# Splitting the second block's input weights early, whole-row convolution taps and shared softmax scalings in a two-block layer on one core

## The chip, the cores and the metric

The kernel runs as one program on one core of a Trainium2 chip. A core has engines that work side by side, each through its own instructions in a fixed order: TensorE (PE: matrix products and transposes), VectorE (DVE), ScalarE (ACT), GpSimd (POOL), and SyncE (SP), which here only issues DMA transfers. The metric is the device time of one execution in microseconds (us). Three runs of the kernel before gave 2321.71, 2323.44 and 2327.45 us, so the median is 2323.44 us.

## The reference

A sequence of 1024 tokens of width 1024 (float32) goes through two blocks. The first normalises the tokens, makes four branches of attention and retention (A to D) from one input product, merges them with gates and adds the result to the input. The second block is the part that the change touches:

```
xn = rms_norm_2(h, g_mix_pre)
z  = xn @ w_in                                   # 1024 x 2308
conf_ab, q, k, v, f_logit, sc_h, sc_b, sc_c, pool_v = split(z)
y_conf = silu(layer_norm(conv31(a * sigmoid(b)))) @ w_conf_pw   # 256 channels, 31 taps, causal
y_att  = forgetting_attention(q, k, v, f_logit + b_forget)      # 4 heads of 64, causal
y_sc   = sc_b * conv3(sc_c * sc_h)                              # 256 channels, 3 taps
y_pool = (windowed mean - v) @ w_pool * scale                   # windows 2, 4, 8, 16
h = h + rms_norm_2(concat(y_conf, y_att, y_sc, y_pool) @ w_out, g_mix_post)
# then a gated MLP and a last gated product
```

## The kernel before

**Products in three parts.** TensorE multiplies float32 values that are split into two parts, hi (the value rounded to the engine's float32r type) and lo (the value minus hi). Each product is hi times hi, hi times lo and lo times hi. The names in the rows are `wr` for a raw weight block from DRAM, `wh` and `wl` for its two parts. One product of 128 output channels by 512 tokens is 24 matmuls of 512 columns into one PSUM bank `mm` (lines 229 to 231).

**Weights.** `load_w` (line 184) loads a weight group block by block through SP's queue into slots of the pool `w` (`NW=9` slots of 128 x 1024 floats), and `split_w` makes hi with ACT or DVE in turn (`WHI='aaav'`, line 147 for ACT's copy, 149 for DVE's cast) and lo with DVE (line 157) or POOL (line 155). A block takes a slot for the raw values and one for each part; in the second block's mixing stage lo is always made by DVE (`WLO2='v'`). For the mixing stage the groups are two for the convolution (conf), two for queries and keys (qk0, qk1), one for values (v, 260 columns, 8 tiles of 128 tokens), two times two for the short convolution (sc, sb) and one for the pooling: 20 raw blocks.

**The stages in time.** Branch D at about 110 to 280 us, branch A at 290 to 660 us, branches C and B to 1000 us, the merges and the first output product to 1178 us, mixing from 1178 to 1512 us, then its output product and the MLP. In the mixing stage the text uses three stretches. Stretch one, 1235 to 1290 us, is the products qk0 and v and the start of the short convolution's product. Stretch two, to 1427 us, is the attention of heads 0 and 1 in eight tiles of 128 queries with other products between them. Stretch three, to 1512 us, is the attention of heads 2 and 3 with the end of the convolution's branch and the first output products.

**The 31 taps.** `tap` (line 1334 in the rows; the first of a channel group at 1331) adds one shifted, weighted copy of `u` to an accumulator on DVE, with both inputs in SBUF. There are two channel groups m and two halves of the tokens, and `conv(m, half)` gives 31 taps each, so 124 instructions of up to 512 columns. `conv_steps` takes from these lists: two taps after each product, four after each attention tile (`CPP=2`, `CS=4`), in turn over the lists of one half; `conv_rest` takes what is left before the convolution's branch is used.

**An attention tile.** `softmax_pair` treats two heads: TensorE makes scores (bank `s`), DVE adds the bias and takes the maximum (line 838, `Pm` and `mx`), combines it (843, 847), ACT makes the exponentials (850), DVE takes the reciprocal of the sum (858) and scales both heads' rows (line 150, `Pm<-Pm,sm`). Then TensorE transposes `Pm` (line 276, bank `t`), ACT and DVE split that into `PT`, TensorE multiplies with the values (816), and DVE and ACT join the result (826, 827).

**Order.** The order on each engine is fixed when the program is built: code is placed in priority order, and a helper `stream` moves a part ahead of or behind the rest. The string `WORK` lists the pieces of the mixing stage one after another. The table `FA` says, for each of branch A's 16 attention tiles, which other pieces follow it.

**The short convolution.** `short_conv` (line 1492) makes sc_h and sc_c, copies sc_h from PSUM with ACT, multiplies with DVE, then makes sc_b, which ACT copies from PSUM, runs three taps of 1024 columns and multiplies by the copy (line 1507).

## Time and profile before

| | |
|---|---|
| runs | 2321.71, 2323.44, 2327.45 us |
| profiled execution, its own time | 2326.04 us |
| its span in the trace | 2324.3 us |
| busy, PE / DVE / ACT / POOL | 2235.5 / 1518.4 / 962.6 / 495.1 us |
| mean granted clock of TensorE | 0.989 of full speed |

TensorE works 96% of the span. In a window from 290 to 660 us it is busy all the time, so other engines' work there is beside it. In the mixing stage it is not: it waits between matmuls, and in windows with such waits the granted clock is below 1.00. A row of a window view has each engine's busy time with its count of instructions, then the clock. A row of a timeline has the start, the duration, the engine, the line, the operation with output and inputs, the count, and in brackets how long the engine had been idle and what released it.

### The profile page before, as it was taken

What the parts mean: (1) busy time and instruction counts of PE and PEld (TensorE: products, weight loads), DVE (VectorE), ACT (ScalarE), POOL (GpSimd) and SP (SyncE); (2) the same over time, 40 slices, a digit from 0 to 9 for tenths busy, and PEclk for the clock granted to TensorE, in tenths of its full rate; (3) what the DMA queues carried; (4) which work ended last, traced back from release to release, by engine and by line L of the source; (5) the groups of instructions that cost most, each with busy time, mean ns of one, the idle gap of its engine ahead of it and who ended that gap; (6) DMA issues with size and microseconds to landing.
All of it is one profiled execution on the core that took longest, in us unless ns stands there. A gap on an engine that the chain in (4) does not pass through costs nothing.

```text
span 2324.3 us, 30295 instructions
## 1 busy us (share of the span) xinstructions
PE 2235.5 (96%) x11004; PEld 1853.1 (80%) x11004; DVE 1518.4 (65%) x2952; ACT 962.6 (41%) x1937; POOL 495.1 (21%) x411
## 2 busy tenths in 40 slices
PE   7999999999989999999998998899999999999998
PEld 6788788888887778877887787677788888888877
DVE  7634466665677965634579876855576778678684
ACT  6211344444455544422322344634445454334452
POOL 4222100010155622224320000012043440000021
PEclk9999999999999999999999999999999999999999
DMA  9432221121132333224320211156555687524313
GB/s 326 154 95 63 60 69 50 49 88 60 33 109 85 115 121 105 73 82 147 107 68 26 82 54 34 37 172 206 161 186 187 197 324 252 181 91 155 117 55 118
DMA packets 202783, 272.72 MB, mean 117 GB/s; under 512 B 17086, under 2 KB 126214, under 8 KB 202634
## 3 DMA queue, kind: packets, MB, share of 16 engines
q1 hardware_dynamic: 194240, 257.95, 34.3%
q10 hardware_dynamic: 8394, 12.84, 1.8%
q8 instruction: 87, 1.43, 0.3%
q14 instruction: 62, 0.51, 0.1%
HBM read 199.43 MB, written 71.32 MB: 116 GB/s over the span
## 4 chain that ended last, share of the span: by engine, by line
PE 46%; DVE 6%; DMA 2%; ACT 1%; issue 1%; POOL 0%; SPq 0%; DVEq 0%; POOLq 0%; ACTq 0%
PE mm L230 6%; PE mm L231 6%; PE mm L229 6%; DVE blk L1334 2%; PE s L1676 2%; PE s L1675 2%; PE s L1674 2%; PE t L2020 1%; PE t L2021 1%; PE t L2019 1%; PE t L276 1%; PE mm L2020 1%; PE t L1676 1%; PE t L1675 1%; PE t L1674 1%; PE mm L2021 1%
## 5 line engine op out<-in xcount | busy, mean ns | idle before, releaser
L229 PE MATMUL mm<-blk,wh 128*128 128x512 f32 x1264 | 506.4, 401 | 12.7 <-DVE tz L1149 5.3
L230 PE MATMUL mm<-blk,wh 128*128 128x512 f32 x1264 | 502.1, 397 | 0.9 <-DVE blk L157 0.9
L231 PE MATMUL mm<-blk,wl 128*128 128x512 f32 x1264 | 501.0, 397 | 2.0 <-POOL wl L155 1.7
L229 PEld LDWEIGHTS mm<-blk,wh 128*128 128x128 f32 x1264 | 239.4, 189 | 65.1 <-DVE tz L1149 7.9
L231 PEld LDWEIGHTS mm<-blk,wl 128*128 128x128 f32 x1264 | 239.4, 189 | 52.4 <-POOL wl L155 2.1
L230 PEld LDWEIGHTS mm<-blk,wh 128*128 128x128 f32 x1264 | 239.5, 189 | 47.8 <-DVE blk L157 1.3
L155 POOL TENSOR_TENSOR wl<-wr,wh 128x1024 fp32r<-128x1024 f32 (+1 forms) x50 | 122.9, 2458 | 480.1 <-ACT wh L147 290.2
L229 PE MATMUL mm<-wh,blk 128*128 128x512 f32 (+3 forms) x544 | 197.0, 364 | 7.1 <-DVE wh L149 1.6
L231 PE MATMUL mm<-wh,blk 128*128 128x512 f32 (+3 forms) x544 | 194.3, 359 | 1.0 <-DVE blk L157 1.0
L157 DVE SCALAR_TENSOR_TENSOR wh<-blk,wh 128x1024 fp32r<-128x1024 f32 x116 | 138.6, 1221 | 66.9 <-issue 59.2
L147 ACT ACTIVATE wh<-blk 128x1024 fp32r<-128x1024 f32 x116 | 117.0, 1053 | 154.4 <-PE s L2020 84.5
L230 PE MATMUL mm<-wl,blk 128*128 128x512 f32 (+3 forms) x480 | 170.2, 355 | 9.5 <-DVE wl L157 9.1
L147 ACT ACTIVATE blk<-mm 64x512 fp32r<-64x512 f32 (+3 forms) x138 | 77.9, 569 | 172.0 <-PE mm L231 113.2
L147 ACT ACTIVATE PT<-t 128x512 fp32r<-128x512 f32 (+3 forms) x224 | 96.0, 460 | 118.2 <-PE o L816 65.9
L147 ACT ACTIVATE wh<-wr 128x1024 fp32r<-128x1024 f32 (+2 forms) x91 | 93.7, 1031 | 102.2 <-DMA wr<-in_w_in_dram 21.9
L157 DVE SCALAR_TENSOR_TENSOR PT<-t,PT 128x512 fp32r<-128x512 f32 (+3 forms) x224 | 111.0, 515 | 37.4 <-ACT PT L147 36.4
L309 POOL TENSOR_TENSOR sm<-sm,mhalf 128x1 f32<-128x1 f32 x64 | 38.8, 610 | 437.3 <-DVE sm L308 422.0
L229 PEld LDWEIGHTS mm<-wh,blk 128*128 128x128 f32 x544 | 103.3, 190 | 25.4 <-DVE wh L149 2.4
L231 PEld LDWEIGHTS mm<-wh,blk 128*128 128x128 f32 x544 | 103.4, 190 | 16.8 <-DVE blk L157 1.9
L230 PEld LDWEIGHTS mm<-wl,blk 128*128 128x128 f32 x480 | 91.7, 191 | 24.3 <-DVE wl L157 11.3
L157 DVE SCALAR_TENSOR_TENSOR wl<-wr,wh 128x1024 fp32r<-128x1024 f32 (+2 forms) x69 | 88.5, 1283 | 31.5 <-PE mm L230 14.0
L1150 POOL TENSOR_TENSOR acc<-tz,acc 128x512 f32<-128x512 f32 x48 | 67.8, 1416 | 132.2 <-DVE tz L1149 86.4
(364 smaller groups left out, 4851.5 us busy)
## 6 DMA issues: line engine op xcount, KB each, us to landing
acc<-acc SPq DMA_DIRECT2D x96, 256.0 KB, 2.6
wr<-in_w_merge_dram SPq DMA_DIRECT2D x32, 512.0 KB, 4.0
wu<-in_w_up_dram SPq DMA_DIRECT2D x32, 512.0 KB, 5.1
blk<-in_w_down_dram SPq DMA_DIRECT2D x32, 512.0 KB, 7.0
blk<-ss SPq DMA_DIRECT2D x32, 512.0 KB, 4.7
wr<-in_w_in_dram SPq DMA_DIRECT2D x27, 512.0 KB, 4.2
ss<-us SPq DMA_DIRECT2D x48, 256.0 KB, 2.3
blk<-sa SPq DMA_DIRECT2D x24, 512.0 KB, 4.3
```

The costliest lines, as they stand in the source:

```text
L147: return ac.activation(dst, src, AF.Copy, scale=1.0 if scale is None else scale)
L155: return po.tensor_tensor(lo, x, hi.bitcast(F32), op=ALU.subtract)
L157: return ve.scalar_tensor_tensor(out=lo, in0=x, scalar=scale, in1=hi.bitcast(F32), op0=ALU.mult, op1=ALU.subtract)
L229: pe.matmul(dst, sh, mh, start=(i == 0), stop=False)
L230: pe.matmul(dst, sh, ml, start=False, stop=False)
L231: last = pe.matmul(dst, sl, mh, start=False, stop=(i == n - 1))
L1150: po.tensor_tensor(acc[:], t[:], acc[:], op=ALU.add)
L1334: ve.scalar_tensor_tensor(out=acc[:, c:c1], in0=u[:, c - l:c1 - l], scalar=w, in1=acc[:, c:c1], op0=ALU.mult, op1=ALU.add)
L1674: pe.matmul(dst, wh, xh, start=first and k == 0, stop=False, skip_group_check=True)
L1675: pe.matmul(dst, wh, xl, start=False, stop=False, skip_group_check=True)
L1676: last = pe.matmul(dst, wl, xh, start=False, stop=k == 3, skip_group_check=True)
L2020: pe.matmul(d, sh[:, c, ts_], tl[:, c, :], start=False, stop=False)
```

## The change

Three edits, and one table that orders them.

First, the 20 raw blocks of `w_in_2` are split during branch A. A generator `w2_split` loads a block by SP's queue, makes hi with ACT and lo with DVE, and stores both parts to DRAM by GpSimd's queue. `FA` gains 20 letters `w`, each one such step, over all 16 tiles (one after most tiles, two after five of them). In the mixing stage `load_w2` loads the parts with GpSimd's queue, 40 loads, in place of 20 raw loads by SP's queue, and nothing is split there.

Second, the taps. Group 0's first 16 taps stay in halves, its other 15 and all 31 of group 1 run over whole rows of 1024 columns: 32 + 15 + 31 = 78 instructions. They stand in a stream of their own, placed 150 priorities later (`TAPL=150`), and the lists are taken one after another.

Third, in the mixing attention the scaling of a tile's first head goes to ACT and that of the second stays with DVE (`NORM2='av'`). With these, `short_conv` makes sc_b after its taps and multiplies straight from PSUM, half by half, so that ACT's copies of sc_b go; and two small casts (`identR`, `causR`) come earlier.

```diff
-FA={(0, 2): 'g', (0, 3): 'mmm', (0, 7): 'qm', (1, 0): 'gg', (1, 6): 'gz'} ... NORM2='v'
+FA={(0, 0): 'w', (0, 1): 'w', (0, 2): 'gw', (0, 3): 'mmmw', ... (1, 0): 'ggww', (1, 1): 'ww', ...} ... NORM2='av', TAPL=150
...
     def conv_steps(n):
-        for _ in range(n):
-            if convs:
-                half, steps_ = convs.pop(0)
-                if next(steps_, "end") != "end":
-                    convs.insert(sum(h == half for h, _ in convs), (half, steps_))
+        with stream("taps", tc.tile_snap_priority() + _T["TAPL"]):
+            for _ in range(n):
+                if convs and next(convs[0], "end") == "end":
+                    convs.pop(0)
...
+    def w2_split():
+        for key, (cs_, n, per) in w2_cols.items():
+            N = n * len(cs_)
+            for b in range(KC // per):
+                raw = main.tile([P, per, N], F32, name=nm("wr"), tag="w", bufs=NW)
+                for i, c0 in enumerate(cs_):
+                    sy.dma_start(raw[:, :, i * n:(i + 1) * n], w_in2[:, b * per:(b + 1) * per, c0:c0 + n])
+                hi, lo = [main.tile([P, per, N], F32R, name=nm("wh"), tag="w", bufs=NW) for _ in range(2)]
+                copy(hi[:], raw[:], "a")
+                sub_lo(lo[:], raw[:], hi[:])
+                for j, t in enumerate((hi, lo)):
+                    d = dram.tile([P, per, N], F32R, name=nm("w2"), tag=nm("w2"), bufs=1)
+                    po.dma_start(d[:], t[:])
+                    w2_d[key, b, j] = d
+                yield
...
+    def load_w2(*key):
...
+        for b in range(KC // per):
+            for j, p_ in enumerate((w.h, w.l)):
+                p_[b] = main.tile([P, per, n * len(cs_)], F32R, name=nm("wh"), tag="w", bufs=NW)
+                po.dma_start(p_[b][:], w2_d[key, b, j][:])
...
-    def conv(m, half):
-
-        for l in range(31):
-            tap(accs[m], us[m], l, dwc[:, m, 30 - l:31 - l], l == 0, half * 512, half * 512 + 512)
+    def conv(m, ls, halves=((0, S),)):
+
+        for l in ls:
+            for c0, c1 in halves:
+                tap(accs[m], us[m], l, dwc[:, m, 30 - l:31 - l], l == 0, c0, c1)
             yield
...
     for m in range(2):
         z_half(hT2, first[m], 1, conf_evac[m])
-        convs.append((1, conv(m, 1)))
+        if m == 0:
+            convs.append(conv(0, range(16), ((512, S),)))
+            convs.append(conv(0, range(16, 31)))
+        else:
+            convs.append(conv(1, range(31)))
...
-            z_group(hT2, load_w([(w_in2[:, :, 1540 + m * P:1540 + (m + 1) * P], 0)], 128),
-                    lambda b, j, half: copy(bb[:, half * 512:(half + 1) * 512], b[:], "a"), ms=(0,))
-            for l in range(3):
-                tap(hh_, u, l, dwc[:, m, 33 - l:34 - l], l == 0)
-            ve.tensor_mul(hh_[:], hh_[:], bb[:])
...
+        for l in range(3):
+            tap(y, u, l, dwc[:, m, 33 - l:34 - l], l == 0)
+
+        def times(b, j, half):
+            cs = slice(half * 512, (half + 1) * 512)
+            ve.tensor_mul(y[:, cs], b[:], y[:, cs])
+        z_group(hT2, load_w2("sb", m), times, ms=(0,))
```

Three places show how the order moves. The first is DVE while TensorE makes the v product, in stretch one; `fl` and the 4x64 rows are that product's results, and line 1334 (before) or 1374 (after) is a tap. Before:

```order
L1334 SCALAR_TENSOR_TENSOR blk_11224<-blk_11312,dwc,blk_11224 128x489
L1334 SCALAR_TENSOR_TENSOR blk_11223<-blk_11225,dwc,blk_11223 128x512
L1334 SCALAR_TENSOR_TENSOR blk_11224<-blk_11312,dwc,blk_11224 128x512
L157 SCALAR_TENSOR_TENSOR blk_11674<-mm_11758,blk_11674 128x4x64
L149 COPY fl<-mm_11758 128x4
L1334 SCALAR_TENSOR_TENSOR blk_11224<-blk_11312,dwc,blk_11224 128x488
```

After:

```order
L1374 SCALAR_TENSOR_TENSOR blk_11435<-blk_11437,dwc,blk_11435 128x994
L157 SCALAR_TENSOR_TENSOR blk_11870<-mm_11919,blk_11870 128x4x64
L149 COPY fl<-mm_11919 128x4
L157 SCALAR_TENSOR_TENSOR blk_11871<-mm_11947,blk_11871 128x4x64
L149 COPY fl<-mm_11947 128x4
L157 SCALAR_TENSOR_TENSOR blk_11871<-mm_11975,blk_11871 128x4x64
L149 COPY fl<-mm_11975 128x4
```

Between two tiles of v stood three to six taps; now the last one stands ahead of the second tile's results, and none comes after them.

The second place is DVE in the attention of heads 0 and 1, around the fifth tile's reciprocal (line 858 before, 903 after; 838 or 883 is a maximum, 826 or 871 and 827 or 872 the joining of an earlier tile's result). Before:

```order
L847 TENSOR_TENSOR sm_12385<-mx_12363,c_63 128x2
L838 ISA Pm_12442,mx_12441<-s_12447,xb_12153 128x256
L838 ISA mx_12441 128x1
L858 RECIPROCAL sm_12390<-sm_12387 128x2
L150 TENSOR_SCALAR Pm_12364<-Pm_12364,sm_12390 128x640
L826 TENSOR_REDUCE blk_12157<-o_12305 64x128
L150 TENSOR_SCALAR Pm_12374<-Pm_12374,sm_12390 128x640
L157 SCALAR_TENSOR_TENSOR wl_12984<-wr_12981,wh_12983 128x1024
```

After:

```order
L1374 SCALAR_TENSOR_TENSOR blk_11436<-blk_11518,dwc,blk_11436 128x1010
L1374 SCALAR_TENSOR_TENSOR blk_11436<-blk_11518,dwc,blk_11436 128x1009
L903 RECIPROCAL sm_12566<-sm_12563 128x2
L871 TENSOR_REDUCE blk_12334<-o_12481 64x128
L1374 SCALAR_TENSOR_TENSOR blk_11436<-blk_11518,dwc,blk_11436 128x1008
L150 TENSOR_SCALAR Pm_12550<-Pm_12550,sm_12566 128x640
L872 TENSOR_TENSOR blk_12334<-blk_12334,ju_12528 128x128
L1374 SCALAR_TENSOR_TENSOR blk_11436<-blk_11518,dwc,blk_11436 128x1007
L883 ISA Pm_12627,mx_12616<-s_12628,xb_12332 128x512
```

One scaling and the weight's subtraction left this row of work, and four taps of whole rows came into it. From the reciprocal of the fourth tile to that of the seventh there are 19 such taps after and none before.

The third place is POOL at the end of the first output product, with the norm's power (`sm`, line 309 before, 308 after), the row sums (`row`, 1267 or 1312) and, after, the loads of weight parts (line 694). Before:

```order
L309 TENSOR_TENSOR sm_11105<-sm_11105,mhalf 128x1
L155 TENSOR_TENSOR wl_11237<-wr_11229,wh_11236 128x1024
L1267 TENSOR_TENSOR row_11144<-xt_11142,row_11144 128x512
L309 TENSOR_TENSOR sm_11113<-sm_11113,mhalf 128x1
L155 TENSOR_TENSOR wl_11324<-wr_11316,wh_11323 128x1024
```

After:

```order
L694 DMA wh_11519<-w_581_2951 128x1024
L308 TENSOR_TENSOR sm_11317<-sm_11317,mhalf 128x1
L694 DMA wh_11521<-w_583_2953 128x1024
L694 DMA wh_11523<-w_691_3574 128x1024
L694 DMA wh_11525<-w_693_3576 128x1024
L694 DMA wh_11735<-w_741_3747 128x1024
L1312 TENSOR_TENSOR row_11356<-xt_11354,row_11356 128x512
L308 TENSOR_TENSOR sm_11325<-sm_11325,mhalf 128x1
```

Two subtractions of weights left POOL, and nine loads came, eight of them together; the last row sums stand behind these.

## Rows read from the trace of the kernel before

**Rows 1.** The page: busy time by engine, then the chain's lines.

```profile
PE 2235.5 (96%) x11004; PEld 1853.1 (80%) x11004; DVE 1518.4 (65%) x2952; ACT 962.6 (41%) x1937; POOL 495.1 (21%) x411
...
PE mm L230 6%; PE mm L231 6%; PE mm L229 6%; DVE blk L1334 2%; PE s L1676 2%; PE s L1675 2%; PE s L1674 2%; PE t L2020 1%; PE t L2021 1%; PE t L2019 1%; PE t L276 1%; PE mm L2020 1%; PE t L1676 1%; PE t L1675 1%; PE t L1674 1%; PE mm L2021 1%
```

**Rows 2.** Windows: length, PE, PEld, DVE, ACT, POOL busy, clock, DMA.

```profile
1235.00:1290.00 55.00, 43.83 (x263) 38.74 (x263) 54.59 (x94) 12.29 (x22) 0.00 (x0) 0.91 0.19 49
1290.00:1427.00 137.00, 134.61 (x678) 112.21 (x677) 99.77 (x218) 51.45 (x108) 2.46 (x3) 1.00 0.17 51
1427.00:1512.00 85.00, 71.94 (x361) 55.22 (x360) 71.47 (x199) 49.47 (x112) 4.36 (x7) 0.94 0.11 38
...
1255.00:1260.00 5.00, 1.97 (x7) 1.67 (x8) 4.94 (x8) 0.98 (x2) 0.00 (x0) 0.55 0.39 101
...
1460.00:1470.00 10.00, 8.79 (x35) 5.23 (x34) 9.99 (x30) 10.00 (x21) 0.93 (x1) 1.00 0.00 1
290.00:660.00 370.00, 370.00 (x2050) 319.86 (x2049) 230.91 (x722) 170.33 (x429) 46.16 (x39) 1.00 0.18 58
```

**Rows 3.** The chain of waits that ended last, 1235 to 1300 us, by line.

```profile
by line: DVE blk L1334 60.5%; DVE blk L157 10.3%; PE mm L231 7.6%; PE mm L229 6.7%; PE mm L230 6.5%; DVE wl L157 3.6%; issue 2.1%; PE t L276 1.3%; DVE fl L149 1.1%; DVE wh L149 0.9%
```

**Rows 4.** Timeline of PE, stretch one: its longest wait.

```profile
1256.94 0.58 PE L230 MATMUL mm<-wl,blk 128*128 128x260 f32 x1 [2.93 <-DVE wl L157]
```

**Rows 5.** Timeline of DVE: taps, a cast and a subtraction, stretch one.

```profile
1261.44 5.94 DVE L1334 SCALAR_TENSOR_TENSOR blk<-blk,dwc,blk 128x512 f32<-128x512 f32 x9
...
1281.45 0.69 DVE L149 CAST wh<-wr 128x1024 fp32r<-128x1024 f32 x1
...
1284.41 1.23 DVE L157 SCALAR_TENSOR_TENSOR wl<-wr,wh 128x1024 fp32r<-128x1024 f32 x1
1285.54 0.73 DVE L1334 SCALAR_TENSOR_TENSOR blk<-blk,dwc,blk 128x482 f32<-128x482 f32 x1
```

**Rows 6.** Line 1334 in stretch one, 1235 to 1290 us: count, durations.

```profile
L1334 DVE SCALAR_TENSOR_TENSOR blk<-blk,dwc,blk x64: 710/740/758, 1234.5 to 1289.9; 128x512 f32<-128x512 f32 x37, 128x491 f32<-128x491 f32 x2, 128x490 f32<-128x490 f32 x2, 128x489 f32<-128x489 f32 x2
```

**Rows 7.** Windows in the attention of heads 0 and 1 (columns as above).

```profile
1338.28:1370.32 32.04, 29.65 (x163) 24.53 (x162) 24.65 (x69) 14.71 (x32) 0.00 (x0) 1.00 0.18 50
1290.00:1338.28 48.28, 48.28 (x232) 39.97 (x231) 37.33 (x78) 16.97 (x38) 0.00 (x0) 1.00 0.21 61
```

**Rows 8.** Timeline of DVE there: the fourth and the seventh tile's reciprocal.

```profile
1338.28 0.17 DVE L858 RECIPROCAL sm<-sm 128x2 f32<-128x2 f32 x1 [1.12 <-ACT Pm L850]
...
1370.32 0.16 DVE L858 RECIPROCAL sm<-sm 128x2 f32<-128x2 f32 x1
```

**Rows 9.** Mixing, by line: DVE's scalings and ACT's copies, durations min/median/max.

```profile
L150 DVE TENSOR_SCALAR Pm<-Pm,sm x32: 279/511/754, 1315.6 to 1499.5; 128x128 f32<-128x128 f32 x4, 128x256 f32<-128x256 f32 x4, 128x384 f32<-128x384 f32 x4, 128x512 f32<-128x512 f32 x4
...
L147 ACT ACTIVATE wh<-wr x17: 623/1057/1065, 1177.1 to 1512.0; 128x1024 fp32r<-128x1024 f32 x14, 128x520 fp32r<-128x520 f32 x3
```

**Rows 10.** DMA issues of 1178 to 1512 us: KB, us to landing.

```profile
wr<-in_w_in_dram SPq DMA_DIRECT2D x4, 512.0 KB, 4.3
...
wr<-in_w_in_dram SPq DMA_DIRECT2D x4, 260.0 KB, 3.0
```

**Rows 11.** Timeline of SP's queue, end of the first output product: one issue.

```profile
1171.92 0.34 SPq L1277 DMA_DIRECT2D x<-row  x1
```

**Rows 12.** Timeline of POOL, same place.

```profile
1172.07 2.41 POOL L155 TENSOR_TENSOR wl<-wr,wh 128x1024 fp32r<-128x1024 f32 x1 [1.50 <-ACT wh L147]
1174.43 1.75 POOL L1267 TENSOR_TENSOR row<-xt,row 128x512 f32<-128x512 f32 x1
```

**Rows 13.** Timeline of DVE and of POOL around 1086 us.

```profile
1085.40 2.74 POOL L155 TENSOR_TENSOR wl<-wr,wh 128x1024 fp32r<-128x1024 f32 x1 [1.21 <-DVE wl L157]
...
1085.80 2.90 DVE L149 CAST wh<-wr 128x1024 fp32r<-128x1024 f32 x1
```

**Rows 14.** Timeline of PE: two matmuls of one product, 512 columns.

```profile
1342.03 0.39 PE L231 MATMUL mm<-blk,wl 128*128 128x512 f32 x1
1342.26 0.39 PE L229 MATMUL mm<-blk,wh 128*128 128x512 f32 x1
```

72 lines of the change are left out of this document (44 added, 28 removed).

## The prediction, made before the changed kernel ran

> **What bounds the kernel now.** I read the page first, then windows, then the waits. TensorE is busy 2235.5 of 2324.3 us and leads the chain; the one DVE line in the chain's list that is worth naming is the taps, 2% [rows 1]. So only places where TensorE waits can give time. The windows show two of them in the mixing stage [rows 2]. In stretch one TensorE works 43.83 of 55.00 us while DVE works 54.59: DVE is the bound, and the chain there is 60.5% taps [rows 3]. TensorE's longest wait, 2.93 us, ends on DVE's weight subtraction [rows 4]. The granted clock is 0.91 over the stretch, and in the 5 us in which TensorE worked only 1.97 it was 0.55 [rows 2], so waits are paid a second time. In stretch three TensorE works 71.94 of 85.00 at clock 0.94, DVE 71.47, and ACT 10.00 of 10 us for a while. In stretch two TensorE works 134.61 of 137.00: nearly nothing to gain, and something to lose.
>
> **Stretch one: gain.** At most the idle 55.00 - 43.83 = 11.2 us and the lost clock, 0.09 x 55 = 5.0, together 16. DVE loses 64 taps of a half row [rows 6]. Nine in a row take 5.94 us, 0.66 each; so 64 x 0.66 = 42.2. Three subtractions of 1.23 and about two half-sized, and a cast of 0.69 [rows 5], go too: 3.7 + 1.4 + 0.7 = 5.8. Fifteen taps of a whole row come; a row of that size is followed by the next start 1.13 us later (1284.41 to 1285.54) [rows 5], so 17 us. DVE then has 54.6 - 42.2 - 5.8 + 17 = 24 us of work beside some 44 of TensorE: it is no longer the bound. What is late next is the weights' slots. Of the nine slots the v group takes eight, and the last of them come free only when qk0 ends; sc0's parts wait for v in the same way. A landing took 3.0 us for a v block and 4.3 for a full one from SP's queue [rows 10], and the last product before it covers part. I leave about 2 us of wait for each and 1 for the clock: 5 of the 16 stay. Gain 11, bounds 3 (each wait a full landing and an issue, and more clock) and 16.
>
> **Stretch two: loss.** The taps of channel group 1 that DVE no longer does in stretch one now stand between the pieces of the softmax. I take the stretch from the fourth to the seventh reciprocal, 1338.28 to 1370.32 us [rows 8], because before and after it the order gives TensorE products to work on, and inside it, after the change, there are none for three tiles. Before, DVE works 24.65 of 32.04 us, TensorE 29.65 [rows 7]. Out of DVE go one subtraction (1.23), one cast (0.70) and one scaling of three tiles (about 0.5 each [rows 9]): 21.2 left. In come 19 whole-row taps at 1.13: 21.5. So DVE has 42.7 us of work. TensorE has less than before, since some 5 us of the filling product moved ahead of the stretch: about 24.6. The difference is 18.1. DVE may enter it ahead; the maxima of a tile can't be taken before its scores, so I allow one tile's spare, 3 us. That gives 15 us of waiting where 2.4 stood: +12.7, and +1.3 for the clock after waits of several us (0.55 in the window named above). Loss 14. Bounds: 4, if DVE arrives some 10 us ahead (in the 48.28 us before the stretch it worked only 37.33 [rows 7], 10.9 spare), and 20, if it has no lead and the clock costs more. Between the ends I go nearer the upper one, because the taps before the stretch stand in the same kind of order and eat that spare time.
>
> **Stretch three: gain.** Eight of the scalings leave DVE, 8 x 0.5 = 4 us [rows 9], with two subtractions and a cast, 3 us more; the waits on the softmax shorten by at most that. ACT takes the eight scalings, and there it is at 10.00 of 10 us [rows 2], so part turns into waiting for ACT. Gain 4, bounds 0 and 12 of the 13.1 idle and 5.1 of clock. The moved scalings of stretch two are counted above; ACT has 51.45 of 137 there, and there they cost nothing.
>
> **The short convolution.** ACT loses four copies per half pair; DVE does two products of half a row from PSUM in place of one whole row, in stretches two and three, where the sum above already lies within the bounds. I cost it at 0; without that cover it is half a microsecond.
>
> **The start of mixing.** Nine loads go to GpSimd's in-order queue; behind eight of them stand the last row sums, the first of which began at 1174.43 [rows 12]. No row shows an issue by GpSimd: the nearest from below is SP's, 0.34 us [rows 11], from above the longest POOL operation there, 2.41 [rows 12]. Eight give 2.7 to 19 us from about 1166, when the first slots come free. Two subtractions of that kind leave POOL in return. I take a value near SP's, as both only start a transfer: the sum is 1 to 2 us later and covered by the convolution's product, which TensorE has ready. With the wait for the first parts I set +1, bounds 0 and 8. A value below nothing is excluded: TensorE did not wait there.
>
> A page speaks against the parts' way through GpSimd. In this trace a cast of 128 x 1024 took 0.69 us alone [rows 5] and 2.90 us while POOL subtracted beside it [rows 13]. The Trainium skill, page "SBUF — State Buffer", section "Who interferes with whom", says that a DVE instruction with two SBUF inputs contends with GpSimd instructions that read SBUF, and that a transfer which DVE seems to stall was one whose descriptors GpSimd makes. The taps are such instructions, and by that rule the loads would start late while taps run; by the row the price of a collision is up to 2.2 us. No run here shows it for a transfer. It is the second rival below.
>
> **Branch A: nothing.** Twenty steps add 20 copies of 1.06 us to ACT [rows 9] and 20 subtractions of 1.23 to DVE [rows 5], 21 and 25 us in a window of 370 in which TensorE works 370.00, DVE 230.9 and ACT 170.3 [rows 2]. DVE goes to 256 of 370, ACT to 191. TensorE's full row hides it. Without that cover, a subtraction ahead of a softmax piece in a quarter of the steps would cost 5 x 1.23 = 6 us; that is the upper bound, and the lower one is 0, as TensorE can't be busier. The 40 stores only hold slots, which the merge weights of the same tiles use too.
>
> **The sum.** -11 + 14 - 4 + 1 + 0 = 0. The profiled execution took 2326.04 us, 2.6 above the median, so the forecast is the median: 2323 us. What is gained where DVE was the bound is paid back where it becomes the bound.
>
> **Rivals.** First, faster: DVE keeps its lead into the attention tiles, the taps fall into its waits for ACT's exponentials, and stretch two loses only its lower bound, 4, while stretch three gains 7: -13 + 4 - 7 + 1 = -15, 2308 us. For it: DVE's spare 10.9 us before the stretch and 7.4 in it. Against it: 19 taps come to 21.5 us. If stretch two lost nothing at all, it would be 2299.
>
> Second, slower: the parts come late through GpSimd's queue. Eight groups (qk0, v, two sc, two sb, the pooling, qk1) follow one another through nine slots. From the point at which issue and landing exceed the 5.5 us of one product (24 matmuls, 0.23 from one start to the next [rows 14]), TensorE waits for each group; with 5 us landings in place of 4.3, an issue of 1 and a collision of 2.2 it would be some 2.5 us per group, 20 us, of which the forecast already has 4 to 5. Price about +13 with the clock: 2336 us. For it: no load of before had to wait for the parts of the group ahead in this way, as raw blocks needed a slot less at a time. Against it: landings of 3.0 and 4.3 us stand well below 5.5.
>
> Third, slower: branch A doesn't hide the splits. +6 and some waiting of merge weights for slots, +4: 2333 us. Against it: 139 us of idle DVE time in that window.
>
> That the change does not do what it says is unlikely: the order shows the taps and loads where it puts them.
>
> **How the numbers follow.** A measurement of this kernel can tell a change of 0.3%, 7 us, from none; so faster is below 2316.5 and slower above 2330.4. The forecast has 0.43: its terms leave it within 2314 to 2332, 0.31 of it same, 0.06 on either side. The first rival has 0.30, all but 0.01 faster (the case at 2299 in it, 0.05). The second has 0.20, the third 0.07, both slower but for 0.01. Faster: 0.06 + 0.29 = 0.35. Same: 0.31 + 0.01 + 0.01 = 0.33. Slower: 0.06 + 0.26 = 0.32. The terms' ends summed would reach -24 and +31; they won't meet, and leaving out a tenth at each end I give 2305 to 2338 us.
>
> **What would show it.** In the changed kernel's windows: DVE well below full in stretch one, with TensorE's waits there ending on transfers into `wh`; in the attention of heads 0 and 1 TensorE waiting some 12 to 17 us on `Pm` and maxima with DVE full, and taps in the chain there instead of in stretch one; branch A with TensorE still full. Wrong it is if TensorE works through these tiles without long waits (then faster), or if waits on transfers appear at each product (then slower).

## The result and the profile after

| | before | after |
|---|---|---|
| median of four runs each on one chip, us | 2323.16 (2321.71 to 2327.45) | 2345.71 (2343.32 to 2352.20) |
| ratio, 95% interval | 1 | 1.0099, 1.0084 to 1.0115 |
| predicted | | 2323, range 2305 to 2338 |

The change costs 22.5 us and lies outside the range. To see where, I take the start of the same instruction in both timelines, seven times along the program, and subtract. The marks are the first scores of branch A, the load of the table for the first sigmoid of branch C, the first maximum of branch B, the first tanh of the convolution's group (mixing), the scan ahead of mixing's attention, the pooling's first shifted sum on DVE, which stands among the tiles of heads 0 and 1, and the first square of the output product behind mixing.

| mark (time before, us) | after | what lies between, and its own change |
|---|---|---|
| A, 278.1 | -1.8 | |
| C, 628.0 | +23.5 | branch A: +25.3 |
| B, 839.1 | +19.9 | branch C: -3.6 |
| mixing, 1190.2 | +20.8 | branch B, merges, start of mixing: +0.9 |
| scan, 1301.8 | +1.3 | stretch one: -19.5 |
| pooling, 1363.6 | +19.6 | attention of heads 0 and 1: +18.3 |
| output product, 1527.3 | +18.2 | the rest of mixing: -1.4 |

Behind the last mark 3.0 more are lost. So mixing itself came out at -2.6, and the loss stands in branch A, which the prediction set at nothing. The marks stand on DVE, ACT and TensorE, and work moves across them, so a part can be off by a few us; the sums over A with C (+21.7) and over mixing are firmer.

The page of after, to be read with [rows 1]:

```profile
PE 2239.3 (95%) x11004; PEld 1856.8 (79%) x11004; DVE 1502.2 (64%) x2889; ACT 977.2 (42%) x1954; POOL 530.9 (23%) x489
...
w<-wh POOLq DMA_DIRECT2D x32, 512.0 KB, 5.0
wh<-w POOLq DMA_DIRECT2D x32, 512.0 KB, 4.9
```

TensorE's busy time grew by 4 us only; the rest is waiting. The windows of after (columns as in [rows 2]), first branch A from mark to mark, with 20 us out of its middle, then branch C, then stretch one and the attention of heads 0 and 1 from mark to mark:

```profile
276.30:651.50 375.20, 364.10 (x1919) 308.76 (x1918) 236.09 (x741) 174.04 (x423) 54.38 (x52) 0.99 0.39 120
...
540.00:560.00 20.00, 16.55 (x88) 13.59 (x87) 14.82 (x51) 10.92 (x27) 3.19 (x6) 0.91 1.01 313
...
651.50:859.10 207.60, 186.09 (x1046) 157.88 (x1045) 153.53 (x216) 108.35 (x236) 105.65 (x108) 0.99 0.31 94
...
1211.00:1303.00 92.00, 89.39 (x483) 76.93 (x483) 59.20 (x89) 15.89 (x31) 12.04 (x22) 0.98 0.28 85
1303.00:1383.00 80.00, 70.34 (x329) 58.08 (x328) 67.73 (x136) 29.02 (x67) 3.19 (x6) 0.89 0.21 69
```

The same stretches of before, which the windows of [rows 2] do not have:

```profile
278.10:628.00 349.90, 349.90 (x1876) 299.53 (x1875) 219.66 (x716) 154.13 (x397) 35.58 (x17) 1.00 0.19 60
...
540.00:560.00 20.00, 20.00 (x103) 16.93 (x102) 11.86 (x44) 8.29 (x21) 2.50 (x1) 1.00 0.26 79
...
1190.00:1302.00 112.00, 100.83 (x519) 85.16 (x518) 105.63 (x175) 23.46 (x40) 3.31 (x4) 0.95 0.15 39
1302.00:1364.00 62.00, 59.61 (x307) 49.55 (x306) 44.25 (x113) 25.26 (x60) 0.00 (x0) 1.00 0.22 60
```

Read the last but one column: between 540 and 560 us the DMA engines went from a share of 0.26 to 1.01, and TensorE from full to 16.55 of 20. Neither ACT nor DVE is near full there (10.92 and 14.82 of 20), so the sum of their added work does not explain it. Over the whole branch TensorE now stands idle for 11.1 us, and the clock takes some 4 (busy time times the missing share of the clock, summed over windows of 10 us). The other 10 of the 25.3 are work that moved: 43 more matmuls lie between the marks (1919 against 1876), and about as many fewer in branch C (1046 against 1088). Branch C gave only 3.6 back for them, as TensorE idles 21.5 us there where it idled 16.2. That is why the sum over A with C is the firmer one.

TensorE's waits in branch A, after, are short and many, and 8.7 of the 11.1 us end on DVE (total us, times, longest); before there are none:

```profile
PE s L842 <- DVE mx L883: 4.4, 5, 2.3
PE mm L229 <- ACT tz L1187: 2.4, 1, 2.4
```

Who waits for what, from the waits of ACT and DVE in branch A, after:

```profile
ACT wh L147 <- DMA wr<-in_w_in_dram: 27.9, 13, 3.6
DVE wh L157 <- ACT wh L147: 13.0, 7, 3.9
```

Before, DVE had no such wait, and ACT's was this:

```profile
ACT wh L147 <- DMA wr<-in_w_in_dram: 1.8, 2, 1.6
```

One of the thirteen, followed through the timeline of after:

```profile
407.19 1.06 ACT L147 ACTIVATE wh<-wr 128x1024 fp32r<-128x1024 f32 x1 [3.60 <-DMA wr<-in_w_in_dram]
408.16 0.58 ACT L1187 ACTIVATE tz<-mm 128x512 f32<-128x512 f32 x1
408.28 1.23 DVE L157 SCALAR_TENSOR_TENSOR wh<-wr,wh 128x1024 fp32r<-128x1024 f32 x1 [3.90 <-ACT wh L147]
...
408.79 0.51 PE L229 MATMUL mm<-blk,wh 128*128 128x512 f32 x1 [2.41 <-ACT tz L1187]
...
411.04 0.63 PE L230 MATMUL mm<-blk,wh 128*128 128x512 f32 x1
```

ACT executes in order. It stands 3.60 us at the copy of a raw block that has not landed; behind that copy is the tanh of a merge product, which frees a PSUM bank, and TensorE waits 2.41 us for that bank. DVE stands 3.90 us at the subtraction behind the same copy. The matmuls from 410 us on take 0.63 instead of 0.39 us [rows 14]: the granted clock, 1.00 up to 409 us, was 0.73 from 409 to 411 and 0.50, the lower of its two levels, from 411 to 413. So this wait is paid again in clock; not every wait is (8.79 of 10 us at 1.00 in [rows 2]). ACT was busy for 174.04 of the branch's 375.20 us, so it had time enough; what was in TensorE's way here was the one instruction at which it stood.

### The profile page after: what moved, and what is told of

Same layout as the page of the kernel before. It is cut to its first block, busy times and chain, and to the rows that moved or that the text cites. A ratio compares the mean times of both kernels' runs of the same rounds, so it can differ in the third digit from the quotient of the medians.

```text
span 2345.5 us, 30416 instructions
## 1 busy us (share of the span) xinstructions
PE 2239.3 (95%) x11004; PEld 1856.8 (79%) x11004; DVE 1502.2 (64%) x2889; ACT 977.2 (42%) x1954; POOL 530.9 (23%) x489
## 4 chain that ended last, share of the span: by engine, by line
PE 44%; issue 4%; DVE 4%; DMA 2%; ACT 1%; POOL 1%; ACTq 0%; DVEq 0%; POOLq 0%; SPq 0%
PE mm L229 6%; PE mm L230 6%; PE mm L231 6%; PE s L1723 2%; PE s L1722 2%; PE s L1724 2%; PE t L275 1%; PE t L2068 1%; PE t L2069 1%; PE t L2067 1%; PE mm L2068 1%; PE t L1723 1%; PE mm L2069 1%; PE t L1722 1%; PE t L1724 1%
## 5 line engine op out<-in xcount | busy, mean ns | idle before, releaser
L229 PE MATMUL mm<-blk,wh 128*128 128x512 f32 x1264 | 505.9, 400 | 17.1 <-DVE tz L1194 6.0
L230 PE MATMUL mm<-blk,wh 128*128 128x512 f32 x1264 | 501.8, 397 | 0.9 <-DVE blk L157 0.9
L231 PE MATMUL mm<-blk,wl 128*128 128x512 f32 x1008 | 400.1, 397 | 1.6 <-POOL wl L155 1.2
L231 PEld LDWEIGHTS mm<-blk,wl 128*128 128x128 f32 x1008 | 190.9, 189 | 41.8 <-POOL wl L155 1.6
L155 POOL TENSOR_TENSOR wl<-wr,wh 128x1024 fp32r<-128x1024 f32 (+1 forms) x48 | 117.0, 2437 | 343.6 <-ACT wh L147 209.7
L230 PE MATMUL mm<-wl,blk 128*128 128x512 f32 (+2 forms) x416 | 150.3, 362 | 4.6 <-DVE wl L157 4.6
L147 ACT ACTIVATE wh<-wr 128x1024 fp32r<-128x1024 f32 (+2 forms) x96 | 98.6, 1028 | 111.3 <-DMA wr<-in_w_in_dram 46.6
L147 ACT ACTIVATE blk<-mm 64x512 fp32r<-64x512 f32 (+3 forms) x130 | 73.0, 567 | 143.5 <-PE mm L231 98.6
L231 PE MATMUL mm<-blk,wh 128*128 128x512 f32 x256 | 100.5, 393 | 0.1
L275 PE MATMUL t<-c,Pm 128*128 128x128 f32 x508 | 83.8, 284 | 13.8 <-ACT Pm L147 8.9
```

The costliest lines, as they stand in the source:

```text
L147: return ac.activation(dst, src, AF.Copy, scale=1.0 if scale is None else scale)
L155: return po.tensor_tensor(lo, x, hi.bitcast(F32), op=ALU.subtract)
L229: pe.matmul(dst, sh, mh, start=(i == 0), stop=False)
L230: pe.matmul(dst, sh, ml, start=False, stop=False)
L231: last = pe.matmul(dst, sl, mh, start=False, stop=(i == n - 1))
L275: pe.transpose(dst, src, ident)
```

## The experiments

Three questions: which edit loses, by what means branch A loses, and what the taps are worth. The table has every run; the intervals are of the ratio to before on the same chip. "A" is how much branch A grew, from its first scores to the mark of branch C, and "A, C" how much both grew, to the mark of branch B, where work that moved between them does not count. Each is read from one profile.

| run | us | ratio, 95% interval | A | A, C |
|---|---|---|---|---|
| after | 2345.71 | 1.0084 to 1.0115 | +25.3 | +21.7 |
| mix_only | 2319.87 | 0.9975 to 0.9997 | 0.0 | 0.0 |
| split_only | 2341.08 | 1.0063 to 1.0107 | +23.1 | +18.6 |
| taps_early | 2341.84 | 1.0067 to 1.0103 | +25.5 | +20.6 |
| mix_taps | 2319.52 | 0.9975 to 1.0001 | -0.1 | +0.5 |
| raw_ahead | 2353.69 | 1.0117 to 1.0147 | +23.8 | +26.8 |
| no_stores | 2333.42 | 1.0030 to 1.0066 | +5.2 | +6.7 |
| no_raw | 2329.50 | 1.0008 to 1.0031 | -0.6 | +3.8 |
| mix_turns | 2314.75 | 0.9959 to 0.9979 | 0.0 | +0.1 |
| const_stores | 2371.73 | 1.0186 to 1.0217 | +5.2 | +7.3 |
| thin_stores | 2334.89 | 1.0030 to 1.0058 | +8.1 | +10.8 |
| turns_halves | 2320.32 | 0.9972 to 0.9991 | 0.0 | +0.3 |
| turns_dve | 2319.57 | 0.9967 to 0.9986 | 0.0 | +0.1 |
| freed_bytes | 2342.07 | 1.0064 to 1.0094 | +22.6 | +19.8 |
| freed_thin | 2334.49 | 1.0029 to 1.0057 | +10.0 | +12.2 |
| spread | 2352.31 | 1.0106 to 1.0146 | +1.7 | +19.3 |
| spread_turns | 2339.06 | 1.0044 to 1.0098 | +1.2 | +19.3 |
| eight_turns | 2320.93 | 0.9977 to 0.9995 | -0.2 | +1.4 |
| fourteen_turns | 2328.38 | 1.0010 to 1.0033 | +1.2 | +4.5 |

**Which edit.** `mix_only` leaves the early split out and keeps the rest; `split_only` has the early split alone.

```diff
 (mix_only, from after)
-FA={(0, 0): 'w', (0, 1): 'w', (0, 2): 'gw', ...
+FA={(0, 2): 'g', (0, 3): 'mmm', (0, 7): 'qm', (1, 0): 'gg', (1, 6): 'gz'} ...
...
     def load_w2(*key):
...
+        return load_w([(w_in2[:, :, c0:c0 + n], i * n) for i, c0 in enumerate(cs_)], n * len(cs_), per=per)
```

> The changed kernel without its first part: no splits in branch A, the mixing stage loads and splits its weights as before; whole-row taps, the scaling on ACT and the short convolution as changed. Theory: branch A alone costs the changed kernel about 20 us, and the rest (stretch one -20, attention of heads 0 and 1 +21, last stretch -3) cancels, so 2322 to 2330 us, with TensorE busy all of branch A. Rival: stretch one's gain came from the early split, not from the taps that left it; then it is about 2335 us, since the loss in the attention stays.

> The kernel before with the early split and the loads of parts alone; taps, scalings and short convolution as before. Theory: branch A loses its 20 us, stretch one gains 5 at most from the subtractions that leave DVE, so about 2338 us (2333 to 2344), and the attention of heads 0 and 1 stays without long waits. Rival: the loss in branch A is of another origin than the split (the order of other pieces); then near 2320.

Without the early split the rest gains a little (0.9986, just below the time that was expected). The early split alone gives 1.0085. From the mixing mark to the scan `mix_only` gained 18.1 us, after 19.5: nearly all of that gain is had without the weights. `split_only` gained 8.1 there, so the two don't add.

**By what means branch A loses.** `raw_ahead` asks for each raw block one step earlier. `no_stores` drops the 40 stores and loads the raw blocks in mixing. `no_raw` keeps the stores and splits one raw block again and again.

```diff
 (raw_ahead)
...
+        ahead = raw_of(*blocks[0])
+        for i, (key, b) in enumerate(blocks):
+            raw, ahead = ahead, raw_of(*blocks[i + 1]) if i + 1 < len(blocks) else None
...
 (no_stores)
...
-                    po.dma_start(d[:], t[:])
...
 (no_raw)
...
+                if not held:
+                    held.append(main.tile([P, 1024], F32, name=nm("wr"), tag="w", bufs=NW))
...
```

> The changed kernel, but each step of the early split asks for the next block's raw values before it copies its own, so that a raw block lands a step ahead. Theory: branch A's loss comes from ACT standing at a copy until the raw block lands (some 2 to 3.6 us at 11 of the 20 copies), with the attention's copies and exponentials behind it; with the block there in time branch A loses 8 us at most and the run is 2328 to 2335 us. Rival: the loss is the added work on ACT and DVE; then 2343 to 2348.

> The changed kernel without the 40 stores: each step loads, copies and subtracts as before, and the mixing stage loads raw blocks in place of both parts (so its result is not the reference's; times and transfers in mixing are the same). Theory: without stores the slots come free at once and the transfers of the raw blocks meet no others; branch A loses 0 to 6 us and the run is 2326 to 2332. Rival (added work): 2343 to 2348.

> The changed kernel with one raw block loaded once and all 20 steps working on it: the copies, subtractions and stores stay, 19 loads go (its result is not the reference's). Theory (ACT waits for the raw block): branch A loses 0 to 4 us, 2324 to 2331. Rival one (added work): 2343 to 2348. Rival two (the stores themselves crowd the other loads of branch A): near 2340.

`no_raw` is the clearest: all copies, subtractions and stores are there, and branch A is 0.6 us shorter than before, A with C 3.8 longer. So the added work on ACT and DVE costs next to nothing, as predicted, and so do stores by themselves. `no_stores` is the other half: raw loads without stores cost 5.2 (6.7 with C). Only both together cost 25 (21.7 with C). Loading earlier missed: branch A lost as much (23.8), and branch C, which in after gives 3.6 back, lost another 3.0. It holds one more of nine slots; that this is why is argued, not shown.

How long ACT stands in all is not the price. With earlier loads its waits for raw blocks fell to 17.9 us, and branch A lost as much; without stores they hardly fell, and it lost little. What did fall in `no_stores` is what DVE waits behind ACT. The same two waits there (276 to 655 us):

```profile
ACT wh L147 <- DMA wr<-in_w_in_dram: 23.5, 16, 3.4
DVE wh L157 <- ACT wh L147: 5.8, 6, 1.3
```

That DVE's standing carries the loss to TensorE fits these two and TensorE's waits above; `raw_ahead` doesn't fit it (6.3 us of DVE's wait, longest 3.4), and no run changed it by itself. The waits of SP's queue in branch A, after, show what its loads of raw blocks stand for most:

```profile
SPq L672 <- DMA w<-wh: 25.6, 6, 6.6
```

That is a raw load waiting for a slot whose part is still being stored. Two explanations were left: a store holds the slot too long, or its bytes delay everything. `thin_stores` stores two columns of each part; `const_stores` stores as many bytes from a tile that holds no slot. `thin_stores`, like `no_stores`, loads raw blocks in mixing.

```diff
 (thin_stores)
...
-                    po.dma_start(d[:], t[:])
+                    po.dma_start(d[:, 0, :2], t[:, 0, :2])
...
 (const_stores)
...
+                    po.dma_start(d[:].rearrange("p a b -> p (a b)"), hT.h[0][j][:].rearrange("p a b -> p (a b)")[:, :per * N])
```

> The changed kernel, except that each of the 40 stores sends two columns of a part and the mixing stage loads the raw blocks in place of the parts. GpSimd issues as many transfers as in the changed kernel, but they carry almost nothing and land at once. Theory, slots or traffic: what the stores cost lies in holding slots or in bytes; branch A is 3 to 9 us late, 2328 to 2336 us. Rival, issues: 40 issues of 0.53 us on GpSimd delay the subtractions of the other weights that stand behind them; then branch A stays 15 to 25 us late and the time is 2340 to 2348 us.

> The changed kernel, except that each of the 40 stores of branch A sends the same number of bytes from a tile of the normalised input, which stays in SBUF for the whole branch, instead of from the part just made. The parts loaded in the mixing stage are therefore other data. The transfers, their queue and GpSimd's issues stay; only the slot of a part is free as soon as the subtraction is done. Theory, slots: branch A was late because a raw block could not start before a store had left a slot; then it is some 5 us late here, as without any stores (there +5 at the first exponential of branch C, here +3 to +10), and the time is 2328 to 2336 us. Rival, traffic: the stores' bytes delay the raw loads themselves; then branch A stays 18 to 25 us late and the time is 2340 to 2348 us.

`thin_stores` says that GpSimd's 40 issues are not the cause (+8.1). `const_stores` missed and did not answer: its stores needed nothing of branch A, so the scheduler issued all 40 ahead of branch D, from 50 to 106 us. The window there, `const_stores` first, then before:

```profile
60.00:120.00 60.00, 29.60 (x112) 22.68 (x113) 8.70 (x22) 8.59 (x15) 26.79 (x44) 0.70 1.04 374
...
60.00:120.00 60.00, 56.73 (x290) 47.02 (x289) 35.63 (x71) 16.42 (x26) 14.95 (x14) 0.94 0.42 140
```

With the DMA engines full (1.04) TensorE worked half the time, branch A began 36.4 us late, and then took only 5.2 longer, as without stores. A pair tied the stores to their place: a small store of the part, then, for `freed_bytes`, a full store from a tile that holds no slot, and for `freed_thin`, which loads raw blocks in mixing, a second small one.

```diff
 (freed_bytes; freed_thin has two columns in the last line too)
...
+                    po.dma_start(d[:, 0, :2], t[:, 0, :2])
...
+                    po.dma_start(d[:].rearrange("p a b -> p (a b)"), hT.h[0][j][:].rearrange("p a b -> p (a b)")[:, :cols_])
```

> The changed kernel, except that in branch A each part is stored in two columns only, which frees its slot after a small landing, and right behind that a full block of the same size as the changed kernel's goes from a tile of the normalised input, which holds no slot, into the same place in DRAM. The parts loaded in mixing are therefore other data. The bytes and their time in branch A are the changed kernel's, the slots' time is not. GpSimd stands for the small landing before each full store. Compared with its pair, which is the same with small stores alone: theory slots: the start of branch C is within 3 us of the pair's, and 5 to 15 us earlier than in the changed kernel (+23.5); 2330 to 2339 us. Rival bytes: the start of branch C is 10 us or more later than the pair's, near +23; 2340 to 2350 us.

> The pair: the same stores and the same waits on GpSimd, but the second store of each part has two columns too, and the mixing stage loads the raw blocks in place of the parts. It carries almost no bytes. Both theories: branch C starts some 6 to 12 us later than before (8.0 with one small store per part), as GpSimd now stands for 40 small landings; 2332 to 2339 us. If it is above 2341 us, GpSimd's standing is the larger cost and the pair tells nothing on slots.

The bytes count: branch A grew by 22.6 us with them and by 10.0 without, and with them nearly as much as in after (25.3), though no full store held a slot. They are not all of it: over A with C it is 19.8 against 12.2, of which 6.7 is there without any store. How, from the DMA issues between 520 and 600 us (KB each, median us to landing), `freed_bytes` first:

```profile
wr<-in_w_in_dram SPq DMA_DIRECT2D x8, 256.0 KB, 5.1
...
w<-wh POOLq DMA_DIRECT2D x20, 1.0 KB, 5.3
```

and `freed_thin`:

```profile
wr<-in_w_in_dram SPq DMA_DIRECT2D x14, 256.0 KB, 3.5
...
w<-wh POOLq DMA_DIRECT2D x20, 1.0 KB, 3.2
```

A raw load of 256 KB lands 1.6 us later, and a store of 1 KB 2.1 us later, beside full stores. The small store holds the slot in both, so slots come free later too. How much of the bytes' price comes by way of slots can't be told from these runs.

Was it the closeness of the stores? `spread` puts eight steps into branch A and six each into C and B; `spread_turns` has the taps in turn as well.

```diff
-FA={(0, 0): 'w', (0, 1): 'w', ...
+FA={(0, 1): 'w', ..., (0, 3): 'mmmw', (0, 5): 'w', (0, 7): 'qmw', (1, 0): 'ggw', (1, 2): 'w', ...
-FC={(0, 3): 'mm', (0, 7): 'q', (1, 3): 'zm', (1, 6): 'm'}
+FC={(0, 1): 'w', (0, 3): 'mmw', (0, 5): 'w', (0, 7): 'q', (1, 1): 'w', (1, 3): 'zmw', (1, 5): 'w', (1, 6): 'm'}
```

> The changed kernel with its 20 steps spread over three branches: eight in branch A (every other tile), six each in branches C and B, in place of 20 in branch A. The same loads, splits and stores. Theory, bunching: the changed kernel lost its time where the steps stood close enough to fill the DMA engines (share 1.01 between 540 and 560 us); spread, the share stays well below 1, the raw blocks come in time, and the first output product starts at most 8 us later than before (+18.3 in the changed kernel): 2326 to 2336 us. Rival, the steps themselves: each step that waits for its raw block in ACT's order costs its microsecond wherever it stands; the first output product starts 14 us or more late, 2340 to 2350 us.

> The same spread, with the taps of the two groups in turn. Theory: taps in turn give what they gave without the early split (some 5 us against taps one group after another), and the early split then gives back what its steps cost at most: 2316 to 2330 us, not below the 2314.75 us of the version without an early split. Rival: with its cost spread away the early split is worth the weights' work it takes from DVE in mixing, 7 us of subtractions in stretch one: 2306 to 2313 us.

In branch A the theory held: eight steps cost 1.7 us, twenty cost 25, where in proportion eight would cost 10. The times missed all the same, that of `spread_turns` both of its ranges, because six steps in branch C cost 17.6 and 18.1. The window of branch C in `spread`, and its waits of POOL:

```profile
632.00:861.00 229.00, 204.26 (x1097) 172.89 (x1095) 171.93 (x234) 119.06 (x252) 112.37 (x128) 0.95 0.48 145
```

```profile
POOL Pm L1149 <- ACT Pm L1146: 48.3, 21, 16.1
POOL w L678 <- ACT wh L147: 31.3, 8, 9.1
```

Before, the same branch:

```profile
628.00:839.00 211.00, 194.83 (x1088) 166.16 (x1087) 159.14 (x224) 111.35 (x244) 107.83 (x109) 0.98 0.30 92
```

The DMA engines are half free (0.48), but here POOL masks what ACT's sigmoids give (line 1149; its wait for them was 48.0 us before), and it stands 31.3 us in order at stores whose part ACT has not made. TensorE's idle time grew from 16.2 to 24.7 us, the clock fell from 0.98 to 0.95. It may be that the same step meets another queue that it holds up. That POOL's standing is the cause here is argued from this profile; no run took it away. So the rival of `spread` came nearer to the time (2352.31; it had 2340 to 2350), by a reason that branch A refutes.

**What the taps are worth.** `taps_early` and `mix_taps` run 47 taps right behind the qk0 product, one with the early split and one without. `mix_turns` is `mix_only` with the taps of the two groups in turn; `turns_halves` cuts its whole rows in halves; `turns_dve` puts both scalings back on DVE.

```diff
 (taps_early, mix_taps)
...
     qk = [qk0]
+    conv_steps(47)
...
 (mix_turns, in conv_steps)
...
-                if convs and next(convs[0], "end") == "end":
-                    convs.pop(0)
+                if convs:
+                    s_ = convs.pop(0)
+                    if next(s_, "end") != "end":
+                        convs.append(s_)
...
 (turns_halves)
...
-                convs.append(conv(1, range(31)))
+                convs.append(conv(1, range(31), ((0, 512), (512, S))))
...
 (turns_dve)
-... NORM2='av' ...
+... NORM2='v' ...
```

> The changed kernel with all taps of both channel groups handed to the order ahead of the v product, so that group 1's stand in stretch one and at most two or three between the first tiles' softmax pieces. Theory: the loss of 21 us in the attention is these taps; DVE has some 20 us to spare beside v, so 2328 to 2334 us. Rival: the loss there comes from the scaling on ACT or from loads through GpSimd's queue; then still about 2345.

> Both of these: no splits in branch A, taps ahead of v. Theory: the two losses are independent, so 2306 to 2314 us, faster than both kernels. Rival: with the subtractions back on DVE in stretch one the taps make it the bound there again, and it is about 2320.

> The changed kernel without the early split, with the taps of the two channel groups in turn, so that two taps in a row never write the same accumulator. Theory: a whole-row tap behind one of its own accumulator starts 1.28 us after it, behind another about 1.14; 30 pairs or more give 4 to 6 us of DVE work, and the taps then stand in stretch one; 2312 to 2318 us. Rival: the place of the taps alone counts, and it is 2319 to 2322, as with the taps ahead of v.

> The version without early split and with the taps of the two groups in turn (2314.75 us), with every tap in two halves in place of whole rows: the order of the taps stays, only their size differs. Theory: a whole row takes 1.22 us in turns and two halves 1.32, so 46 rows in two halves cost DVE 4 to 5 us, some of it in stretches where DVE is the bound: 2316 to 2320 us. Rival: DVE is no longer the bound there and the halves are free: 2313 to 2316 us.

> The version without early split and with the taps in turn (2314.75 us), with both scalings of a tile on DVE again, as before the change. Theory: DVE is what TensorE waits for in the attention of heads 0 and 1, and 8 us of scalings come back to it in the two stretches of attention: 2317 to 2323 us. Rival: ACT is the tighter of the two in the last stretch (it was busy 10.00 of 10 us for a while before the change), and its eight scalings there cost what they save: 2312 to 2316 us.

Moving all 47 taps forward missed in both runs. The loss from the scan to the pooling's mark fell to 3.6 us in `mix_taps` and to 0.9 in `taps_early` (15.3 and 18.3 without the move), so it was the taps'; but the bound moves back into stretch one, whose gain fell to 6.0 and to 8.2 (18.1 and 19.5). `mix_taps` came out where its rival had it. Taps in turn split them between the two stretches. The windows of `mix_turns`, stretch one and heads 0 and 1:

```profile
1187.00:1293.00 106.00, 97.63 (x511) 83.29 (x510) 96.00 (x126) 23.47 (x40) 1.34 (x2) 0.97 0.16 41
1293.00:1356.50 63.50, 60.89 (x311) 50.41 (x310) 46.50 (x112) 26.98 (x62) 0.00 (x0) 1.00 0.21 59
```

Stretch one is 5.5 us shorter than before, and the attention no longer pays: TensorE idles 2.6 us in it, as before (2.4), against 9.7 in after. At 2314.75 us (0.9969) this version beats both kernels; the early split is not in it. From the mixing mark to the output product `mix_turns` gains 7.0 us, `turns_halves` 6.6 and `turns_dve` 4.0. Read so, whole rows are worth next to nothing there, and ACT's share of the scalings about 3 us. The times (2314.75, 2320.32, 2319.57) are of two chips, and the intervals of the ratios overlap, so these sizes rest on one profile each and are not shown.

**Is the early split worth anything?** `spread_turns` gained 17.5 us in mixing against 7.0 of `mix_turns`. If that were the parts' doing, few steps in cheap places should pay. `eight_turns` splits only the blocks of stretch one early, in eight tiles of branch A; `fourteen_turns` adds six blocks in branch B.

```diff
 (eight_turns, from spread_turns)
...
+    early = [("qk", 0), ("v", 0), ("sc", 0)]
...
-        for key, (cs_, n, per) in w2_cols.items():
+        for key in early:
+            cs_, n, per = w2_cols[key]
...
+        if key not in early:
+            return load_w([(w_in2[:, :, c0:c0 + n], i * n) for i, c0 in enumerate(cs_)], n * len(cs_), per=per)
...
 (fourteen_turns)
...
-    early = [("qk", 0), ("v", 0), ("sc", 0)]
+    early = [("qk", 0), ("v", 0), ("sc", 0), ("sb", 0), ("qk", 1), ("sc", 1), ("sb", 1)]
```

> Taps in turn, and only the eight blocks whose parts stretch one needs (qk0, v, the first pair of the short convolution) split early, in eight tiles of branch A; the other twelve are split in mixing as before the change. Theory: eight steps in branch A cost 2 us (1.7 in spread), and in mixing the early parts give most of the 10 us by which spread_turns gained more there than mix_turns (17.5 against 7.0), some 6 us of it in stretch one; 2308 to 2313 us, below mix_turns. Rival: what the early parts gave in spread_turns was time that its late arrival in mixing gave back, not the parts; then the eight steps are a loss of 2 us: 2314 to 2319 us.

> The same with fourteen blocks (qk0, v, both pairs of the short convolution with their single ones, qk1), eight steps in branch A and six in branch B, none in branch C. Theory: six steps in branch B cost 2 us more (2.0 in spread), and the attention stretches lose six more subtractions and casts: 2307 to 2314 us, within 3 us of eight_turns. Rival: stores and loads of branch B meet its own traffic at the merges, and the cost is as in branch C (17.6): 2322 us or more.

Both missed. In `eight_turns` the steps cost branch A nothing (-0.2) and mixing gained 9.4 us, 2.4 more than in `mix_turns`, yet its time (0.9986) is no better than that of `mix_turns` (0.9969); the execution in its profile took 2317.18 us, 3.8 below its median. `fourteen_turns` is slower than before (1.0022): in its profile branch B grew by 8.5 us and mixing gained 6.9, but that execution took 2336.53 us, 8 above its median. So neither eight nor fourteen early blocks give the 17.5 of `spread_turns`. That a late arrival in mixing finds some of its work done already is the other explanation; against it, `fourteen_turns` arrived 18.6 us late and gained no more than `mix_turns`. The six blocks that neither run splits early, those of the convolution and the pooling, are left untested, and the cause of the 17.5 stays open. To the first output product six steps in branch B cost 2.0 in `spread` and 8.5 in `fourteen_turns`, to the mixing mark 6.0 and 8.5. With that execution behind the 8.5, no price of a step in branch B is shown.

## Why the prediction was wrong

**Branch A: nothing. This step failed.** It set added busy time against idle time: DVE to 256 of 370, ACT to 191, "TensorE's full row hides it". `no_raw` shows that this reckoning was right as far as it went. What it left out is that a copy on an in-order engine also waits for its input, and that loads and stores meet at the DMA engines. Its bound, 6 us, priced only subtractions ahead of a softmax piece. The wait for a raw block was not priced at all, and the stores were said to "only hold slots". Measured: 25.3 us for the branch, 21.7 with C, with TensorE idle for 11.1 us where its row was to stay full; 5.2 without the stores, -0.6 without the raw loads, 10.0 with stores of a few bytes in place of 22.6 with full ones. So raw loads and the bytes of the stores together are the price, through engines that stand in order; by which of their waits it reaches TensorE is shown for single waits only. The row that should have warned was there: 0.18 of the DMA engines in use at 58 GB/s [rows 2]. Sixteen raw blocks of 512 KB, four of 260 and two stores of each make 28 MB in all; in a branch that moved 58 GB/s x 370 us = 21 MB, that more than doubles the traffic (120 GB/s after). And it came in bunches: by the timeline of POOL, six of the 40 stores were issued ahead of branch A's mark, and 24 between 510 and 589 us.

**The third rival** was this place at +10, with a chance of 0.07. It named subtractions and slots; the 139 us of idle DVE time held against it did not bear on the question. A wait takes an engine's place in the queue, not its idle time.

**Stretch one: gain 11, bounds 3 and 16; measured 19.5** from mark to mark, of which 10.5 are gained. DVE went from 105.63 of 112 us to 59.20 of 92, and TensorE's idle time from 11.2 to 2.6 us, so it is no longer the bound, as forecast. The waits that I allowed for slots, 2 us for each of two groups, came to one of 0.8. TensorE's waits there, after:

```profile
PE mm L229 <- ACT blk L147: 1.1, 1, 1.1
PE mm L230 <- DMA wh<-w: 0.8, 1, 0.8
PE mm L229 <- DVE fl L149: 0.6, 1, 0.6
```

Idle time (-8.6) and clock (-1.9, reckoned as above) make 10.5 of the 19.5, close to the forecast 11; the rest is TensorE's work that now stands behind the mark (483 matmuls for 519).

**Stretch two: loss 14, bounds 4 and 20; measured 18.3** from the scan to the pooling's mark, of which 12.7 are lost. The mechanism was right. TensorE's waits in the attention of heads 0 and 1, after:

```profile
PE t L275 <- ACT Pm L147: 4.8, 2, 4.4
PE s L842 <- DVE mx L883: 3.7, 3, 1.9
```

They end on `Pm` and on maxima, as written. Idle time grew by 7.3 us (2.4 to 9.7) and the clock took 5.4, together 12.7; the rest is work from stretch one (329 matmuls for 307). So the sum came near, but its two sizes were off in opposite directions, and that is in part luck. From the fourth to the seventh reciprocal, 32.04 us before [rows 8], the timeline of after has

```profile
1341.53 0.17 DVE L903 RECIPROCAL sm<-sm 128x2 f32<-128x2 f32 x1
...
1381.27 0.16 DVE L903 RECIPROCAL sm<-sm 128x2 f32<-128x2 f32 x1
```

39.74 us, +7.7 where 14 was forecast. All of TensorE's waiting lies between these two, 7.3 us more than before where +12.7 was forecast; the clock took 5.4 us, not 1.3: 0.89 from the scan to the mark.

**Stretch three and the start of mixing.** From the first reciprocal of heads 2 and 3 to the last mark -4.5, forecast -4. The start of mixing, taken from the first output product to the mixing mark, +2.5, forecast +1. Both within their bounds.

**The second rival, late parts through GpSimd's queue,** did not come. A 512 KB part landed in 4.9 us, as the rival supposed (5), but TensorE's longest wait for a part in all of mixing was 0.8 us. The section of the Trainium skill that the prediction weighed ("SBUF — State Buffer", "Who interferes with whom") says that a DVE instruction with two SBUF inputs contends with GpSimd instructions that read SBUF. That taps would hold back the loads was the prediction's own step from there: the same section has it that `tensor_tensor`, which reads two inputs, did not stall a transfer when that was tried. With that the 0.8 us agree. The rival's sum is off too: 20 us less the 4 to 5 in the forecast are some 15, not 13, and its clock comes on top. So is the first rival's case at 2299: -13 - 7 + 1 makes 2304.

So mixing was forecast at -1 after its start and measured at -2.6. Nearly all of the miss is the one term put at zero. Of the faster rival, `mix_turns` shows half: heads 0 and 1 lose next to nothing once the taps stand in turn, but then stretch one gains 5.5 us, not 13.

## What to carry to other kernels

Work "hidden" beside a full engine is hidden only if every queue it joins can pass it: before moving it, ask of each new instruction what it waits for, and who stands behind it on its engine. Price a moved transfer by the bytes per microsecond of its place, not by its mean over the program; eight steps in branch A cost 1.4 us over A with C (`eight_turns`), twenty cost 21.7. Work that bounds one stretch is best split over the stretches that have room, in small pieces, rather than pushed whole into the next.

## What the runs showed of the hardware

Taps that write the accumulator of the tap ahead of them are slower than taps in turn. From the timeline of DVE, after, one accumulator:

```profile
1239.97 5.47 DVE L1374 SCALAR_TENSOR_TENSOR blk<-blk,dwc,blk 128x512 f32<-128x512 f32 x7
...
1259.16 3.86 DVE L1374 SCALAR_TENSOR_TENSOR blk<-blk,dwc,blk 128x1003 f32<-128x1003 f32 x3
```

and `mix_turns`, two accumulators in turn:

```profile
1254.99 4.80 DVE L1368 SCALAR_TENSOR_TENSOR blk<-blk,dwc,blk 128x1001 f32<-128x1001 f32 x4
```

A row of such a view divided by its count gives the time of one tap: half a row takes 0.78 us behind its own accumulator and 0.66 in turn [rows 5]; a whole row 1.29 and 1.20. The prediction's 1.13 for a whole row, read from a different pair of neighbours, was 12% short, and whole rows one after another (1.29) save nothing against two halves in turn (1.32).

GpSimd's issue of a load of a part took 0.53 to 0.61 us, between the two bounds (0.34 and 2.41) and near the lower one, as supposed (durations in ns, min/median/max):

```profile
L694 POOL DMA_DIRECT2D wh<-w x39: 527/547/610, 1186.7 to 1412.5; - x39
```
